# Output projection's first part emitted directly behind the queries' projection; the second gated norm's sums and row placed behind the scores of the second query block

## The chip, the cores and the metric

The kernel runs on one core of one Trainium2 chip. The metric is the device time of one execution in microseconds (us). Five engines of the core matter: TensorE (PE in the profile; its weight loads are PEld), VectorE (DVE), ScalarE (ACT), GpSimd (POOL) and SyncE (SP), which here issues the DMAs.

## The reference

A trunk of two layers over 512 tokens of width 1024, in float32. Each layer: RMSNorm, one input projection, two groups of heads side by side (dilated-window attention with 8 query and 2 key/value heads, and a Mamba-2 scan with 16 heads in 2 groups), one output projection of both results added to the residual; then RMSNorm, a SwiGLU feed-forward and a second addition. The part that the change touches, cut from the mixer:

```python
attn = dilated_attention(q, k, v).reshape(bsz, s, ATTN_WIDTH).astype(h.dtype)
y = ssd_chunked(xs, dt, a_neg, bm, cm) + d_skip.astype(jnp.float32)[:, None] * xs.astype(jnp.float32)
y = y.reshape(bsz, s, SSM_INNER).astype(h.dtype) * jax.nn.silu(z)
gsize = SSM_INNER // SSM_GROUPS
y = rmsnorm(y.reshape(bsz, s, SSM_GROUPS, gsize), ssm_norm.reshape(SSM_GROUPS, gsize))
y = y.reshape(bsz, s, SSM_INNER)
return jnp.concatenate([attn, y], axis=-1) @ w_out
```

The gated norm has two groups of 512 channels, each normalised by itself. The output projection has 1536 rows: 512 of the attention, 512 of the first group and 512 of the second.

## The kernel before

Activations lie transposed: channels on the 128 partitions, the 512 tokens along the free axis. The residual is eight tiles `hT[0..7]` of 128x512. A float32 product is made of three products in a shorter float format: each operand is split in a high part (a cast on ScalarE) and a low part (a subtraction on VectorE), and high by high, low by high and high by low are added up in one PSUM accumulator. `split_x` makes the pair `xh`, `xl` of an activation, `split_w` the pair `whi`, `wlo` of a weight tile. `block` multiplies one weight tile with its activations: 12 products of 512 columns for a tile of the output projection, six in one planner operation.

The order of the work is not the order of the code. The code adds operations to a `Plan`, each with its engine, an estimated duration, the tiles that it reads and writes, and a priority: the value that `at(t)` set last, in estimated us, or for `block` the value of `clock[0]`, which each of its products advances. `schedule` then runs a list schedule with these durations: whenever an engine is free, the ready operation with the lowest priority (then with the lowest number, the order in which it was added) goes next, if the buffers that it opens are to be had. SP takes its loads strictly by priority and number. The instructions are emitted in the resulting order, each engine runs its own in that order, and semaphores are set from the tiles that they share. A dependency that only the planner knows makes no semaphore.

PSUM has three accumulators `acc`, two `hold` and three `tr` for transposes and small products. 56 buffers of 128x512 in SBUF (tag `g`) hold the activations; an operation may not take the last 6 of them if one with a priority lower by over 6 still waits for its first.

A layer goes through: the input projection, with the scan's chunks (`ssd`) and gates (`gate`) of both groups spread over it; the queries' projection, whose end in the program's clock is `tq` (L972); `ssd(1)` and `gate(1, tq + 2)` (L974, L975); the attention, for the query blocks 3, 2, 1, 0 (L1033 to L1035); and the output projection, in three parts of eight blocks each, in the order r = 1 (first scan group), 2 (second scan group), 0 (attention) (L1040). `scores(i, ta)` takes its heads in four pairs: scores of two heads in a `tr` and an `acc`, row minimum with the mask added on VectorE (L1004), exponential with its sum on ScalarE, reciprocal and multiplication on VectorE. `values` transposes the result on TensorE, copies it on ScalarE (`pt`) and multiplies it with the values into a `hold`; at its end the block is split into `ath` and `atl`. Neither of them changes `clock[0]`.

`gate(g, ta)` (L909) multiplies the scan's output with the gate on GpSimd and adds up the squares; `nrm.spread()` (L917) then makes the norm's row: TensorE sums the squares over the partitions (`tr<-ones,sq`), VectorE scales them (`var`), GpSimd takes the power (`rcol`), TensorE transposes the result into a full tile, ScalarE copies it (`rstd`). Four multiplications on GpSimd (`xbc<-xbc,rstd`) apply it, and `split_y` (L921) makes the activations of the projection from them, `xh` on ScalarE and `xl` on VectorE (L435).

Of the kernel before, what the change touches and what calls it, by code (L numbers as in the profile page):

```python
# [15 lines left out]
ALU = mybir.AluOpType  # L16
# [3 lines left out]
P = 128  # L20
# [200 lines left out]
class Plan:  # L221
# [32 lines left out]

    def schedule(self, reserve, near):
# [105 lines left out]
def hybrid_trunk(  # L361
# [105 lines left out]
    def mms(outs, prods, each, prio=None):  # L467

        ins = [v for p in prods for v in p[1:3]]

        def fn():
            for p in prods:
                if len(p) == 3:
                    nc.tensor.transpose(R(p[0]), R(p[1]), R(p[2]))  # L474
                else:
                    nc.tensor.matmul(R(p[0]), R(p[1]), R(p[2]), start=p[3], stop=p[4])  # L476
        plan.add("pe", each * len(prods), outs, ins, fn, prio, lat=0.08)
# [94 lines left out]
    class Norm:  # L572
# [13 lines left out]
        def col(self):  # L586
            t = tr()
            mms([t], [(t[:, i:i + 1], self.ss[:, i * P:(i + 1) * P], ones[:, 0:1], True, True) for i in range(NT)],
                0.45)
            v = small([P, NT], "var", 4)  # L590
# [5 lines left out]
        def spread(self):  # L596
            self.col()
# [50 lines left out]
    def pcol(c):  # L648
        return prm[:, c:c + 1]
# [80 lines left out]
    def layer(l, xs, norm):  # L730
# [178 lines left out]
        def gate(g, ta):  # L909
# [7 lines left out]
            nrm.spread()  # L917
# [17 lines left out]
        gate(0, tx[1] + 2)  # L935
# [39 lines left out]
        gate(1, tq + 2)  # L975
# [58 lines left out]
        for n_, i in enumerate((3, 2, 1, 0)):  # L1034
            values(i, scores(i, ta + 9 * n_), ta + 9 * n_ + 6)  # L1035


        ys = {}
        xs_f, norm_f = [], Norm(KD)
        for r in (1, 2, 0):  # L1040
            if r:
                xo = split_y(r - 1, clock[0] - 6)
            else:
                xo = ats
            po = []
            for c0 in (0, 512):
                if r == 0:
                    wv = w_out[l, 0:512, c0:c0 + 512].rearrange("(v g c) n -> v c g n", v=2, g=4)
                    po += chunk([(slice(v * 64, v * 64 + 64), wv[v]) for v in range(2)], 4, 512)
                else:  # L1050
                    po += rows(w_out[l], r * 512, 4, c0, 512)
            for k in range(KD):
                t = block([(po[k], xo, 0, 4)])
                tt("dve", hT[k], hT[k], t, ALU.add)
                if r == 0:
                    xs_f.append(split_x(hT[k], pcol(PC_FFN + l * 8 + k)))
                    norm_f.square(hT[k])
# [241 lines left out]
```

## Time and profile before

| | us |
|---|---|
| median of 3 runs | 1298.68 |
| lowest, highest | 1298.63, 1300.33 |
| the profiled execution | 1299.57 |
| its span, first to last instruction | 1297.8 |
| TensorE, VectorE busy in the span | 1281.8, 992.2 |
| ScalarE, GpSimd busy in the span | 677.9, 139.2 |

The profile is of one execution, by the hardware profiler. Times count from its first instruction. Busy time is the union of an engine's instructions; matmuls are pipelined and their ends modelled, so TensorE's pace is read better from the starts of successive products. The chain is the work that ended last, followed back from release to release. The mean granted TensorE clock of the execution is 0.998 of full speed.

### The profile page before, as it was taken

The numbers are of one execution on the slowest core, as the hardware profiler recorded it, in microseconds if no ns is written. First come the engines' busy times: TensorE is split into PE (matmuls) and PEld (weight loads), VectorE is DVE, ScalarE is ACT, GpSimd is POOL, SyncE is SP. The second block draws the span as 40 slices with busy tenths as digits, with TensorE's granted clock in tenths as the row PEclk, the third lists the DMA queues.
The fourth block names the chain that finished last, engine by engine and source line by source line (L and its number), as shares of the span: only waits on it lengthen the run. The fifth ranks groups of instructions, "written<-read, shape, count | busy, mean of one in ns | idle before, by whom it ended". The sixth has DMA issues, their size and how long they took to land.

```text
span 1297.8 us, 18639 instructions
## 1 busy us (share of the span) xinstructions
PE 1281.8 (99%) x7316; PEld 1077.6 (83%) x7316; DVE 992.2 (76%) x1678; ACT 677.9 (52%) x1070; POOL 139.2 (11%) x109
## 2 busy tenths in 40 slices
PE   9999999999999999999999999999999999999997
PEld 8877776678889989989888777766788899899896
DVE  7987779668667958959879676886786598597694
ACT  8677656556324524424647686465553244254254
POOL 1013454000000000000000234520000000000000
PEclk9999999999999999999999999999999999999999
DMA  7222221123233233242332222111332432332421
GB/s 242 70 65 66 65 66 65 33 66 98 96 116 113 82 114 98 82 135 70 107 98 78 85 65 65 34 65 33 98 98 82 128 110 80 122 98 74 138 98 65
DMA packets 105736, 115.69 MB, mean 89 GB/s; under 512 B 4656, under 2 KB 95024, under 8 KB 105648
## 3 DMA queue, kind: packets, MB, share of 16 engines
q1 hardware_dynamic: 105504, 114.23, 28.1%
q8 instruction: 58, 0.95, 0.3%
q14 instruction: 30, 0.25, 0.1%
q10 hardware_dynamic: 144, 0.26, 0.1%
HBM read 112.39 MB, written 2.10 MB: 88 GB/s over the span
## 4 chain that ended last, share of the span: by engine, by line
PE 89%; DVE 6%; POOL 1%; ACT 1%; issue 1%; DMA 1%; POOLq 0%; ACTq 0%
PE acc L476 68%; PE hold L476 10%; PE tr L476 7%; PE tr L474 3%; DVE wlo L424 2%; DMA raw<-in_w_up_dram 1%; DVE xbc L435 0%; POOL xbc L424 0%; DVE xl L424 0%; DVE hT L424 0%; DVE sa L430 0%; POOL qr L424 0%; ACT whi L461 0%; DVE xl L435 0%; DVE sa L1004 0%
## 5 line engine op out<-in xcount | busy, mean ns | idle before, releaser
L476 PE MATMUL acc<-xh,whi 128*128 128x512 f32 (+1 forms) x1552 | 562.9, 363 | 3.1 <-DVE hT L424 1.8
L476 PE MATMUL acc<-xl,whi 128*128 128x512 f32 (+1 forms) x1552 | 550.8, 355 | 0.2 <-DVE xl L424 0.2
L476 PE MATMUL acc<-xh,wlo 128*128 128x512 f32 (+1 forms) x1536 | 544.6, 355 | 0.0
L461 ACT CAST whi<-raw 128x1024 fp32r<-128x1024 f32 (+3 forms) x248 | 205.4, 830 | 291.6 <-PE acc L476 266.6
L476 PEld LDWEIGHTS acc<-xh,whi 128*128 128x128 f32 x1552 | 293.8, 189 | 54.2 <-issue 11.8
L476 PEld LDWEIGHTS acc<-xh,wlo 128*128 128x128 f32 x1536 | 290.5, 189 | 42.0 <-DVE wlo L424 0.3
L476 PEld LDWEIGHTS acc<-xl,whi 128*128 128x128 f32 x1552 | 293.9, 189 | 37.3 <-issue 0.7
L424 DVE TENSOR_TENSOR wlo<-raw,whi 128x1024 fp32r<-128x1024 f32 (+2 forms) x240 | 237.4, 994 | 17.6 <-ACT whi L461 17.0
L424 DVE TENSOR_TENSOR hT<-hT,acc 128x512 f32<-128x512 f32 x104 | 71.1, 685 | 110.9 <-PE acc L476 110.2
L461 ACT CAST whi<-wsum 128x1024 fp32r<-128x1024 f32 x64 | 67.2, 1050 | 84.4 <-PE tr L476 40.4
L424 DVE TENSOR_TENSOR wlo<-wsum,whi 128x1024 fp32r<-128x1024 f32 x64 | 78.1, 1221 | 14.3 <-ACT whi L461 14.0
L476 PE MATMUL hold<-xh,wlo 128*128 128x256 f32 x256 | 72.6, 283 | 0.3 <-DVE wlo L424 0.3
L476 PE MATMUL hold<-xh,whi 128*128 128x256 f32 x256 | 72.5, 283 | 0.0
L476 PE MATMUL hold<-xl,whi 128*128 128x256 f32 x256 | 72.4, 283 | 0.0
L594 POOL TENSOR_TENSOR rcol<-var,nhalf 128x4 f32<-128x4 f32 x8 | 8.1, 1018 | 563.6 <-DVE var L430 559.0
L463 ACT ACT_TABLE_LOAD x49 | 62.9, 1283 | 5.0 <-DVE xbc L435 3.0
L435 DVE SCALAR_TENSOR_TENSOR xbc<-cu,prm,xbc 128x511 f32<-128x511 f32 (+2 forms) x72 | 58.2, 815 | 0.8
L463 ACT ACTIVATE sa<-sa,mx 128x512 f32<-128x512 f32 (+3 forms) x64 | 36.0, 563 | 26.2 <-DVE mx L1004 26.2
L476 PEld LDWEIGHTS hold<-xh,wlo 128*128 128x128 f32 x256 | 49.1, 192 | 0.5 <-DVE wlo L424 0.5
L476 PEld LDWEIGHTS hold<-xh,whi 128*128 128x128 f32 x256 | 49.1, 192 | 0.5
L476 PEld LDWEIGHTS hold<-xl,whi 128*128 128x128 f32 x256 | 49.1, 192 | 0.5
L424 DVE TENSOR_TENSOR wsum<-raw 128x512 f32<-128x512 f32 x64 | 42.2, 686 | 1.2 <-DMA raw<-in_w_up_dram 0.9
(231 smaller groups left out, 1834.9 us busy)
## 6 DMA issues: line engine op xcount, KB each, us to landing
raw<-in_w_in_dram SPq DMA_DIRECT2D x24, 1024.0 KB, 5.1
raw<-in_w_gate_dram SPq DMA_DIRECT2D x22, 1024.0 KB, 5.2
raw<-in_w_up_dram SPq DMA_DIRECT2D x22, 1024.0 KB, 5.2
raw<-in_w_down_dram SPq DMA_DIRECT2D x24, 768.0 KB, 4.8
raw<-in_w_out_dram SPq DMA_DIRECT2D x8, 1024.0 KB, 5.1
raw<-in_w_out_dram SPq DMA_DIRECT2D x8, 512.0 KB, 6.5
hT<-in_xT_dram SPq DMA_DIRECT2D x8, 256.0 KB, 4.8
raw<-in_w_down_dram SPq DMA_DIRECT2D x4, 512.0 KB, 3.6
```

Source lines behind the costliest of these rows:

```text
L424: lambda: ENG[eng].tensor_tensor(R(o), R(a), R(b), alu))
L435: lambda: nc.vector.scalar_tensor_tensor(R(o), R(a), R(s), R(b), op0, op1))
L461: nc.scalar.copy(R(o), R(a))
L463: nc.scalar.activation(R(o), R(a), func, **kw)
L474: nc.tensor.transpose(R(p[0]), R(p[1]), R(p[2]))
L476: nc.tensor.matmul(R(p[0]), R(p[1]), R(p[2]), start=p[3], stop=p[4])
L594: lambda: nc.gpsimd.tensor_tensor(R(self.r), R(v), R(nhalf), ALU.pow))
```

## The change

`gate` no longer makes the row; a new function `gated` does, with the four multiplications. The first group calls it at once, as before. For the second group it is called after the scores of the second query block in the order (i = 2), with the priority that stands then (`tq + 16` instead of `tq + 2`), and the planner is told (`follow`) that the sums come behind the last multiplication of these scores. The projection's parts are a function `project(r)`; part r = 1 is called before the attention, the parts 2 and 0 behind it.

```diff
--- before.py
+++ after.py
@@ -251,6 +251,12 @@
             d.users.append(o)
         self.ops.append(o)
         return o
+
+    def follow(self, o, d):
+
+        if d not in o.deps and d is not o:
+            o.deps.add(d)
+            d.users.append(o)
 
     def schedule(self, reserve, near):
 
@@ -474,7 +480,7 @@
                     nc.tensor.transpose(R(p[0]), R(p[1]), R(p[2]))
                 else:
                     nc.tensor.matmul(R(p[0]), R(p[1]), R(p[2]), start=p[3], stop=p[4])
-        plan.add("pe", each * len(prods), outs, ins, fn, prio, lat=0.08)
+        return plan.add("pe", each * len(prods), outs, ins, fn, prio, lat=0.08)
 
     def load(o, src, kb, eng="sp"):
         plan.add(eng, max(0.47, kb / 351.0), [o], [], lambda: ENG[eng].dma_start(R(o), src), lat=2.0)
@@ -583,18 +589,20 @@
             else:
                 tt(eng, self.ss, self.ss, s, ALU.add)
 
-        def col(self):
+        def col(self, follow=None):
             t = tr()
-            mms([t], [(t[:, i:i + 1], self.ss[:, i * P:(i + 1) * P], ones[:, 0:1], True, True) for i in range(NT)],
+            o = mms([t], [(t[:, i:i + 1], self.ss[:, i * P:(i + 1) * P], ones[:, 0:1], True, True) for i in range(NT)],
                 0.45)
+            if follow is not None:
+                plan.follow(o, follow.tile.writer)
             v = small([P, NT], "var", 4)
             ts("dve", v, t[:, 0:NT], 1.0 / (P * self.n), EPS, ALU.mult, ALU.add)
             self.r = small([P, NT], "rcol", 4)
             plan.add("pool", 0.96, [self.r], [v, nhalf],
                      lambda: nc.gpsimd.tensor_tensor(R(self.r), R(v), R(nhalf), ALU.pow))
 
-        def spread(self):
-            self.col()
+        def spread(self, follow=None):
+            self.col(follow)
             t = tr()
             tposes(t, [(t[:, i * P:(i + 1) * P], self.r[:, i:i + 1].broadcast_to([P, P]), ident) for i in range(NT)])
             self.row = G("rstd")
@@ -914,7 +922,10 @@
                 act(z[j], z[j], AF.Silu)
                 tt("pool", xbc[j], xbc[j], z[j], ALU.mult)
                 nrm.square(xbc[j], E_ADD)
-            nrm.spread()
+            return nrm
+
+        def gated(g, nrm, follow=None):
+            nrm.spread(follow)
             for j in range(g * 4, g * 4 + 4):
                 tt(E_ROW, xbc[j], xbc[j], nrm.row, ALU.mult)
 
@@ -932,7 +943,7 @@
             for i in range(4):
                 z[g * 4 + i] = scaled(block([(pz[i], xs, 0, KD)]), "z")
         ssd(0, tx[0], tx[1])
-        gate(0, tx[1] + 2)
+        gated(0, gate(0, tx[1] + 2))
 
 
         A = {"q": []}
@@ -972,7 +983,30 @@
         tq = clock[0]
 
         ssd(1, tx[1] + 3, tq)
-        gate(1, tq + 2)
+        nrm1 = gate(1, tq + 2)
+
+
+        xs_f, norm_f = [], Norm(KD)
+
+        def project(r):
+            if r:
+                xo = split_y(r - 1, clock[0] - 6)
+            else:
+                xo = ats
+            po = []
+            for c0 in (0, 512):
+                if r == 0:
+                    wv = w_out[l, 0:512, c0:c0 + 512].rearrange("(v g c) n -> v c g n", v=2, g=4)
+                    po += chunk([(slice(v * 64, v * 64 + 64), wv[v]) for v in range(2)], 4, 512)
+                else:
+                    po += rows(w_out[l], r * 512, 4, c0, 512)
+            for k in range(KD):
+                t = block([(po[k], xo, 0, 4)])
+                tt("dve", hT[k], hT[k], t, ALU.add)
+                if r == 0:
+                    xs_f.append(split_x(hT[k], pcol(PC_FFN + l * 8 + k)))
+                    norm_f.square(hT[k])
+        project(1)
 
 
         ats = []
@@ -1032,29 +1066,13 @@
 
         ta = tq
         for n_, i in enumerate((3, 2, 1, 0)):
-            values(i, scores(i, ta + 9 * n_), ta + 9 * n_ + 6)
-
-
-        ys = {}
-        xs_f, norm_f = [], Norm(KD)
-        for r in (1, 2, 0):
-            if r:
-                xo = split_y(r - 1, clock[0] - 6)
-            else:
-                xo = ats
-            po = []
-            for c0 in (0, 512):
-                if r == 0:
-                    wv = w_out[l, 0:512, c0:c0 + 512].rearrange("(v g c) n -> v c g n", v=2, g=4)
-                    po += chunk([(slice(v * 64, v * 64 + 64), wv[v]) for v in range(2)], 4, 512)
-                else:
-                    po += rows(w_out[l], r * 512, 4, c0, 512)
-            for k in range(KD):
-                t = block([(po[k], xo, 0, 4)])
-                tt("dve", hT[k], hT[k], t, ALU.add)
-                if r == 0:
-                    xs_f.append(split_x(hT[k], pcol(PC_FFN + l * 8 + k)))
-                    norm_f.square(hT[k])
+            pr = scores(i, ta + 9 * n_)
+            if n_ == 1:
+                gated(1, nrm1, pr[-1])
+            values(i, pr, ta + 9 * n_ + 6)
+
+        for r in (2, 0):
+            project(r)
 
 
         at(clock[0])
```

## Rows read from the trace of the kernel before

**Rows 1.** The page: busy us (share) xinstructions; the chain's shares by engine.
```profile
PE 1281.8 (99%) x7316; PEld 1077.6 (83%) x7316; DVE 992.2 (76%) x1678; ACT 677.9 (52%) x1070; POOL 139.2 (11%) x109
...
PE 89%; DVE 6%; POOL 1%; ACT 1%; issue 1%; DMA 1%; POOLq 0%; ACTq 0%
```

**Rows 2.** Windows: stretch, length, busy us (instructions) of PE, PEld, DVE, ACT, POOL; clock.
```profile
203.00:217.00 14.00, 12.39 (x66) 8.92 (x66) 13.41 (x29) 9.93 (x20) 8.06 (x7) 1.00 0.16 62
217.00:240.00 23.00, 23.00 (x132) 15.17 (x131) 17.20 (x57) 14.63 (x38) 0.00 (x0) 1.00 0.15 46
240.00:256.00 16.00, 16.00 (x88) 10.67 (x87) 10.74 (x43) 9.79 (x30) 0.00 (x0) 1.00 0.31 68
```

**Rows 3.** Timeline of TensorE: start us, us, operation, xcount [idle before <-releaser].
```profile
203.04 0.94 PE L476 MATMUL tr<-ones,sq 128*128 128x1 f32 x8
204.37 0.50 PE L476 MATMUL acc<-xh,whi 128*128 128x512 f32 x1 [0.38 <-DVE mx L1004]
204.71 0.40 PE L476 MATMUL acc<-xl,whi 128*128 128x512 f32 x1
...
205.63 0.39 PE L476 MATMUL acc<-xh,wlo 128*128 128x512 f32 x1
205.95 0.50 PE L476 MATMUL tr<-kh,xh 64*128 64x512 f32 x1
206.66 0.50 PE L476 MATMUL acc<-kh,xh 64*128 64x512 f32 x1 [0.21 <-DVE hT L424]
207.27 0.49 PE L476 MATMUL tr<-kh,xl 64*128 64x512 f32 x1
...
207.92 0.50 PE L476 MATMUL acc<-xh,whi 128*128 128x512 f32 x1
```

**Rows 4.** Timeline of TensorE: four transposes and the product behind them, both layers.
```profile
214.34 0.66 PE L474 MATMUL tr<-ident,sa 128*128 128x128 f32 x4
215.90 0.50 PE L476 MATMUL acc<-xh,whi 128*128 128x512 f32 x1 [0.91 <-DVE hT L424]
...
230.55 0.66 PE L474 MATMUL tr<-ident,sa 128*128 128x128 f32 x4
230.96 0.47 PE L476 MATMUL acc<-xh,whi 128*128 128x512 f32 x1
...
856.86 0.50 PE L476 MATMUL acc<-xh,whi 128*128 128x512 f32 x1 [0.92 <-DVE hT L424]
```

**Rows 5.** Timeline of VectorE: first addition of the projection, fourth query block read.
```profile
196.93 0.69 DVE L424 TENSOR_TENSOR hT<-hT,acc 128x512 f32<-128x512 f32 x1 [0.24 <-PE acc L476]
...
198.31 0.68 DVE L435 SCALAR_TENSOR_TENSOR qr<-acc,rstd 128x512 f32<-128x512 f32 x1
```

**Rows 6.** Timeline of VectorE: the norm's var and the low parts.
```profile
207.13 0.15 DVE L430 TENSOR_SCALAR var<-tr 128x4 f32<-128x4 f32 x1
...
213.47 1.78 DVE L435 SCALAR_TENSOR_TENSOR xl<-xbc,prm,xh 128x512 fp32r<-128x512 f32 x1
...
217.91 1.41 DVE L435 SCALAR_TENSOR_TENSOR xl<-xbc,prm,xh 128x512 fp32r<-128x512 f32 x2
```

**Rows 7.** Timeline of GpSimd: the norm's power and its four multiplications.
```profile
207.36 1.02 POOL L594 TENSOR_TENSOR rcol<-var,nhalf 128x4 f32<-128x4 f32 x1 [2.30 <-DVE den L1008]
210.72 5.67 POOL L424 TENSOR_TENSOR xbc<-xbc,rstd 128x512 f32<-128x512 f32 x4 [2.33 <-ACT rstd L461]
```

**Rows 8.** Timelines: block two's last multiplication on VectorE, part 2's first product on TensorE.
```profile
237.07 0.42 DVE L430 TENSOR_SCALAR sa<-sa,den 128x384 f32<-128x384 f32 x1
...
239.72 0.47 PE L476 MATMUL acc<-xh,whi 128*128 128x512 f32 x1
```

**Rows 9.** Timeline of ScalarE: the norm's row copied, the first high part.
```profile
210.05 0.59 ACT L461 COPY rstd<-tr 128x512 f32<-128x512 f32 x1
...
212.05 0.72 ACT L463 ACTIVATE xh<-xbc,prm 128x512 fp32r<-128x512 f32 x1 [0.22 <-POOL xbc L424]
```

**Rows 10.** Groups of TensorE from 239.7 to 252.7: one form of three.
```profile
L476 PE MATMUL acc<-xh,whi 128*128 128x512 f32 x10 | 4.2, 421 | 0.0
```

## The prediction

> **What bounds the kernel now.** I read the page's busy times first, then the chain that ended last, and then the stretches around the moved code. TensorE is busy 99% of the span and is 89% of the chain [rows 1]. A moved step is therefore worth only the time in which TensorE stands still, or in which it changes between kinds of product. The reader is to see next that the place of the old norm is where VectorE is full: 13.41 of 14 us from 203 to 217, with TensorE at 12.39 of 14, while from 217 to 240 and from 240 to 256 VectorE has 5.8 and 5.3 us to spare and TensorE none [rows 2]. Both layers run this stretch alike, the second 640.95 us later (stalls at 215.90 and 856.86 [rows 4]), so everything below is counted per layer and doubled.
>
> **Part one, the first part of the projection.** In the planner an operation is ordered by its priority, and for these blocks that is the TensorE clock of the program, which neither `scores` nor `values` advances. The clock at which part 1 was emitted in the old loop is thus the one right after the queries' projection, as in the new place. The trace agrees: the first addition of a block into hT is at 196.93, before the accumulator of the fourth query block has even been read (198.31) [rows 5]. Only the numbers that decide ties change; there is one equal priority, the first six products of part 1 against the first scores. Its weight loads keep their priorities as well, so no DMA passes another on SP's queue. I cost this part at 0; its bound is one such group exchanged with its neighbour, six products that start 0.23 us apart (four of them from 204.71 to 205.63 [rows 3]), 1.4 us either way.
>
> **Part two, what leaves the old place.** Eight records of the sums (0.94 us at 203.04), the row's transposes, VectorE's var, GpSimd's power (1.02) and four multiplications (5.67 together), ScalarE's copy of the row and four casts, and VectorE's four `xl` [rows 3, 6, 7]. The queues behind them: GpSimd does nothing else from 217 to 256 [rows 2], so its five instructions pass nobody there; SP has no part in them.
>
> (a) The stall at 215.90. VectorE's first `xl` takes 1.78 us where the next two take 1.41 together, until 215.25 [rows 6], and the addition into hT, which sets an accumulator free, stands behind it on VectorE. TensorE's next product waits for that addition [rows 4]. From the four transposes at 214.34 to the product at 215.90 pass 1.56 us; the same pair of steps at 230.55 takes 0.41 [rows 4]. Loss 1.15 us, and it should go, since `xl` leaves this place: -1.15, bounded by 0 if another VectorE instruction takes its turn. What is late next there are scores' own row minima and multiplications, and VectorE, relieved of some 4 us, has them earlier.
>
> (b) The stall at 205.95. Six score products in pairs should take three steps of 0.33, as 207.27 to 207.92 does for two, so 0.98; they took 1.97, because the accumulator waited for hT's addition and the next pair for a query block's `xl` [rows 3]. None of that work is moved. I take 0; the bounds are 0 and -1.0.
>
> (c) The sums' own time. At the old place the product behind them waits another 0.38 us for a row minimum [rows 3], so without the sums TensorE reaches that wait earlier and gains nothing, whereas at the new place, where it is never idle, they cost what they last. +0.94, bounded by 0 if they fall into a wait again. The transposes of the row, four as short as those at 230.55, cost the same in both places: 0.
>
> (d) The new wait. The old order left the second part of the projection long slack: the second and third `xl` are done at 219.32, its first product runs at 239.72 [rows 6, 8]. Now the sums are ordered behind the last multiplication of the second query block's scores, which ended at 237.49 [rows 8]; it may come some 2 us earlier by (a) and by the rooms that the sums and the row no longer take in the scarce transposing buffers. From sums to the second `xl` is a chain: 0.94 + 0.15 + 1.02 + 0.41 + 0.59 + two multiplications of 1.42 + 0.72 + 0.71 = 7.4 us without any handing over [rows 3, 4, 6, 7, 9], and 16.3 as it ran before (203.04 to 219.32). So the first product of part 2 can come between 243 and 254, instead of 239.7. In the 13 us from 239.7 part 2 had 30 products (ten of each of three forms), 0.23 us apart 6.9 us [rows 10]; that is what TensorE lacks if nothing replaces it, the upper bound. What replaces it are the scores of the third query block and the values of the second, which ran between them before, and the last blocks of part 1, which yield to scores that are ready earlier. I take a little, +0.4, because ready attention work is there for most of the gap; bounds 0 and +6.9. Whether the cover is enough hangs on VectorE and ScalarE, which from 240 to 256 are at 10.74 and 9.79 of 16 [rows 2].
>
> (e) Changes of kind. A plain product starts 0.23 us after its like, but scores with 64 rows start 0.32 us after a plain product (205.63 to 205.95 [rows 3]): 0.1 us for a passage, which I take for both directions. With part 2 held back, attention pieces stand side by side, and my estimate is two visits to plain products less, four passages: -0.4, bounds 0 and -0.8.
>
> GpSimd's multiplications hold up VectorE: beside them an `xl` took 1.78 us, after them 0.71 each, 1.07 us lost [rows 6]. The Trainium skill (SBUF — State Buffer, Who interferes with whom) says that a VectorE instruction with two operands in SBUF waits for a GpSimd instruction that reads SBUF, the one that started first keeping the ports to its end. By that rule the 1.07 us is moved with the multiplications, onto the chain of (d), and (d) would be +1.4, the total 2.0 us more; by the row alone it could be the full queue of the old place that made `xl` long. The trace leans to the rule, which makes the second rival dearer.
>
> Sum per layer: 0 - 1.15 + 0 + 0.94 + 0.4 - 0.4 = -0.21, for two layers -0.4. The profiled execution took 1299.57 (span 1297.8 and 1.8 around it), so 1299.15 in its place; the median of the runs is 0.89 below the profiled one, which gives 1298.3.
>
> **The rivals.** *It helps.* VectorE's relief also takes half of (b), the sums fall into a wait and nothing is waited for in (d): -1.15 - 0.5 - 0.4 = -2.05 per layer, -4.1 in all, 1294.6. For it: VectorE is at 96% in the old place and near 70% in the new [rows 2]. Against it: (b) happens before the first instruction that leaves VectorE, `var` at 207.13 [rows 6].
>
> *It hurts.* TensorE's order is written by the planner, with durations of its own; if GpSimd, ScalarE and VectorE bring `xl` later than the planner thought, the first product of part 2 stands in its place and everything behind it waits. That products wait in order is seen at 206.66, where scores wait for an addition and all behind them with it [rows 3]. Price: half of the 6.9 us, 3.4, in place of the 0.4: -1.15 + 0.94 + 3.4 - 0.4 = +2.8 per layer, 5.6 in all, 1304.3. It decides from 1.9 us of waiting per layer on (then the sum is +2.6). For it: 20 us of slack turn into nearly none. Against it: attention work ran without an idle moment between the products of part 2. The Trainium skill (TensorE: Matmul & The Clock Gate, Step-by-step: what each phase is for) has it that the queue pulls only weight loads ahead and keeps the matmuls in program order; the row at 206.66 agrees.
>
> *It does nothing.* Part one is a renumbering, and of part two the planner's new order ends level to within a few tenths: 1298.7. The first is nearly certain by [rows 5], the second a matter of luck.
>
> **How the numbers follow.** Forecast 0.38, no effect 0.08, it helps 0.29, it hurts 0.25. From no change a measurement of this kernel can tell about 0.2%, 2.6 us (its three runs lie 1.7 us apart). Forecast and no effect lie within that, the other two outside: faster 0.29, same 0.46, slower 0.25. Range: (a) whole, (b) gone and (c) hidden give, with (e), -2.55 per layer, 1293.6; the hurting case reaches 1304.3, and its bound of +6.9 goes far beyond. I leave a tenth out on each side: 1293.6 to 1304.5. The likeliest's own range is 1296 to 1301.
>
> **What would show it.** The sums should stand behind the last 384-column multiplication, at some 235 to 238, in the trace. Right for (a): no idle of 0.9 us before a product near 215, and VectorE from 203 to 217 below 12 us. For (b): the pair at 206 still slow. For (d): the start of part 2's first product against the end of part 1's last addition, and TensorE's idle between 238 and 252; more than 1.9 us in each layer shows the hurting rival. The forecast falls if TensorE's idle changes elsewhere, where this change should reach nothing.

## The result, and the profile after

| | before | after |
|---|---|---|
| median of the runs, us | 1299.51 (4 runs) | 1307.78 (4 runs) |
| lowest to highest | 1298.63 to 1302.46 | 1305.76 to 1309.12 |
| the profiled execution, its span | 1299.57, 1297.8 | 1307.41, 1305.6 |

The ratio is 1.0058, with the interval [1.0044, 1.0071]: the change costs some 8 us. It lies above the forecast of 1298.3 and above the whole range, which ended at 1304.5. Lines are 6 higher in the helpers of the changed kernel (the product L476 is L482, `xl` L435 is L441) and the row minimum L1004 is L1038.

The page after, the rows that answer to [rows 1]: the same numbers of instructions, with busy times within 2 us of those before, in a span 7.8 us longer.

```profile
PE 1281.8 (98%) x7316; PEld 1077.1 (82%) x7316; DVE 990.3 (76%) x1678; ACT 678.0 (52%) x1070; POOL 138.3 (11%) x109
...
PE 90%; DVE 6%; DMA 1%; ACT 1%; issue 1%; POOL 1%; POOLq 0%; ACTq 0%
```

The windows of [rows 2], after (columns as there):

```profile
203.00:217.00 14.00, 11.81 (x50) 8.51 (x48) 10.85 (x26) 6.58 (x14) 2.62 (x2) 0.88 0.20 75
217.00:240.00 23.00, 23.00 (x133) 15.13 (x132) 15.89 (x58) 15.93 (x42) 0.00 (x0) 1.00 0.14 46
240.00:256.00 16.00, 13.50 (x76) 8.37 (x76) 11.18 (x37) 9.68 (x25) 6.50 (x5) 1.00 0.01 2
```

VectorE is relieved in the first window, as forecast (10.85 for 13.41), and yet TensorE got through 50 records in place of 66 there (twelve of the 66 are the sums and the row's transposes, which moved); in the third 76 in place of 88. Two places, then, not one. What TensorE waited for between 185 and 285 (in all, times, longest), after and then before:

```profile
PE acc L482 <- DVE hT L430: 2.2, 1, 2.2
PE acc L482 <- DVE xl L441: 2.0, 2, 1.3
PE tr L480 <- DVE sa L436: 0.5, 1, 0.5
PE tr L482 <- DVE xl L430: 0.4, 1, 0.4
```

```profile
PE acc L476 <- DVE hT L424: 1.1, 2, 0.9
PE acc L476 <- DVE mx L1004: 0.4, 1, 0.4
```

**The first place.** TensorE before, the first score product; then after, the same product, the waits for a query block's `xl` and for `hT`, and the wait for `hT` of layer 1:

```profile
190.25 0.50 PE L476 MATMUL tr<-kh,xh 64*128 64x512 f32 x1
```

```profile
193.28 0.49 PE L482 MATMUL tr<-kh,xh 64*128 64x512 f32 x1
...
201.87 0.50 PE L482 MATMUL tr<-kh,xl 64*128 64x512 f32 x1 [0.42 <-DVE xl L430]
...
203.82 0.39 PE L482 MATMUL acc<-xh,wlo 128*128 128x512 f32 x1
206.40 0.50 PE L482 MATMUL acc<-xh,whi 128*128 128x512 f32 x1 [2.19 <-DVE hT L430]
...
207.50 0.63 PE L482 MATMUL acc<-xh,whi 128*128 128x512 f32 x1
207.92 0.63 PE L482 MATMUL acc<-xl,whi 128*128 128x512 f32 x1
...
849.52 0.50 PE L482 MATMUL acc<-xh,whi 128*128 128x512 f32 x1 [2.00 <-DVE hT L430]
```

Before, the first pair of scores ran at 190.25, behind six products of 512 columns; now it runs behind eighteen, 3.03 us later. From 203.82 to 206.40 pass 2.58 us where a step between such products takes 0.23: 2.35 lost. Behind this standstill seven products start 0.43 us apart, 0.20 lost with each, 1.40. In layer 1 the standstill is there too (2.17 lost between 847.13 and 849.52), but not the slow products.

**The second place.** TensorE, GpSimd and VectorE after, around part 2's first products:

```profile
239.66 0.95 PE L482 MATMUL tr<-ones,sq 128*128 128x1 f32 x8
240.54 1.09 PE L482 MATMUL hold<-pt,vk 128*64 128x512 f32 x4
...
246.50 0.49 PE L482 MATMUL acc<-xh,whi 128*128 128x512 f32 x1
248.29 0.50 PE L482 MATMUL acc<-xl,whi 128*128 128x512 f32 x1 [1.29 <-DVE xl L441]
...
249.99 0.50 PE L482 MATMUL acc<-xl,whi 128*128 128x512 f32 x1 [0.73 <-DVE xl L441]
...
251.52 0.33 PE L480 MATMUL tr<-ident,sa 128*128 128x128 f32 x1 [0.47 <-DVE sa L436]
```

```profile
241.19 1.02 POOL L602 TENSOR_TENSOR rcol<-var,nhalf 128x4 f32<-128x4 f32 x1 [34.65 <-DVE var L436]
243.90 5.48 POOL L430 TENSOR_TENSOR xbc<-xbc,rstd 128x512 f32<-128x512 f32 x4 [1.68 <-ACT rstd L467]
```

```profile
246.48 1.75 DVE L441 SCALAR_TENSOR_TENSOR xl<-xbc,prm,xh 128x512 fp32r<-128x512 f32 x1
...
248.75 1.18 DVE L441 SCALAR_TENSOR_TENSOR xl<-xbc,prm,xh 128x512 fp32r<-128x512 f32 x1
...
251.38 0.74 DVE L441 SCALAR_TENSOR_TENSOR xl<-xbc,prm,xh 128x512 fp32r<-128x512 f32 x1
```

Over the usual steps TensorE loses 1.56, 0.90 and 0.64 us here, 3.10 in layer 0, and 3.08 in layer 1. The first two losses are waits for part 2's `xl`, 2.46 together; the third is a wait for a multiplication `sa` of the third query block.

**Where the time went.** The same instruction of the scan or of the projection, start after minus start before, is the measure: +0.30 ahead of layer 0's attention, +5.22 behind its output projection, +3.69 ahead of layer 1's attention, +5.82 behind its projection, +7.76 in the feed-forward of layer 1. So the mixer of layer 0 costs 4.92 us: 2.35 and 0.58 (a wait for a query block's `xl` at 201.87) and 1.40 at the first place, 3.10 at the second, less 2.57 for the stalls of before (0.52, 0.71, 0.27 and 1.07), which are gone; that makes 4.86. Layer 1's costs 2.13: 2.17 and 3.08 less 2.90, 2.35. The -1.5 between them is a stretch from 773 to 777 in which the trace of before has its products at half rate, and that of after has not; the +1.9 at the end are waits for the low parts of weights (1.16 at 1040.83). Neither of these two follows the change: of the experiments' profiles some have them and some have not. Nor does the 1.40 of slow products belong to the change for certain, since experiment 3's trace has the same wait at the same place and no slow products.

### The profile page after: what moved, and what is told of

Same layout as the page of the kernel before. It is cut to its first block, busy times and chain, and to the rows that moved or that the text cites. A ratio compares the mean times of both kernels' runs of the same rounds, so it can differ in the third digit from the quotient of the medians.

```text
span 1305.6 us, 18639 instructions
## 1 busy us (share of the span) xinstructions
PE 1281.8 (98%) x7316; PEld 1077.1 (82%) x7316; DVE 990.3 (76%) x1678; ACT 678.0 (52%) x1070; POOL 138.3 (11%) x109
## 4 chain that ended last, share of the span: by engine, by line
PE 90%; DVE 6%; DMA 1%; ACT 1%; issue 1%; POOL 1%; POOLq 0%; ACTq 0%
PE acc L482 69%; PE hold L482 10%; PE tr L482 8%; PE tr L480 3%; DVE wlo L430 1%; DMA raw<-in_w_up_dram 1%; DVE xl L441 1%; DVE xbc L441 0%; DVE sa L1038 0%; DMA w<-in_w_in_dram 0%; POOL xbc L430 0%; DVE sa L436 0%; DVE xl L430 0%; POOL sq L430 0%; ACT whi L467 0%
## 5 line engine op out<-in xcount | busy, mean ns | idle before, releaser
L482 PE MATMUL acc<-xh,whi 128*128 128x512 f32 (+1 forms) x1552 | 562.8, 363 | 4.3 <-DVE hT L430 4.2
L482 PE MATMUL acc<-xl,whi 128*128 128x512 f32 (+1 forms) x1552 | 552.0, 356 | 4.3 <-DVE xl L441 4.0
L482 PE MATMUL acc<-xh,wlo 128*128 128x512 f32 (+1 forms) x1536 | 545.3, 355 | 0.0
L482 PEld LDWEIGHTS acc<-xh,whi 128*128 128x128 f32 x1552 | 294.2, 190 | 55.2 <-issue 9.7
L482 PEld LDWEIGHTS acc<-xl,whi 128*128 128x128 f32 x1552 | 294.3, 190 | 43.2 <-DVE xl L441 5.5
L482 PEld LDWEIGHTS acc<-xh,wlo 128*128 128x128 f32 x1536 | 290.9, 189 | 41.5 <-DVE wlo L430 0.3
L482 PE MATMUL hold<-xh,wlo 128*128 128x256 f32 x256 | 72.8, 284 | 1.8 <-DVE wlo L430 1.8
L482 PE MATMUL hold<-xh,whi 128*128 128x256 f32 x256 | 72.5, 283 | 0.0
L482 PE MATMUL hold<-xl,whi 128*128 128x256 f32 x256 | 72.4, 283 | 0.0
L441 DVE SCALAR_TENSOR_TENSOR xbc<-cu,prm,xbc 128x511 f32<-128x511 f32 (+2 forms) x72 | 58.2, 815 | 0.8
L482 PEld LDWEIGHTS hold<-xh,wlo 128*128 128x128 f32 x256 | 49.1, 192 | 2.4 <-DVE wlo L430 2.4
L482 PEld LDWEIGHTS hold<-xh,whi 128*128 128x128 f32 x256 | 49.1, 192 | 0.5
L482 PEld LDWEIGHTS hold<-xl,whi 128*128 128x128 f32 x256 | 49.1, 192 | 0.5
```

Source lines behind the costliest of these rows:

```text
L441: lambda: nc.vector.scalar_tensor_tensor(R(o), R(a), R(s), R(b), op0, op1))
```

## The experiments

All in five rounds, each with its own runs of the kernel before beside it (medians 1299.3 to 1300.3). Times in us; "layer 0" is the shift against before behind that layer's output projection.

**1. The two parts by themselves.** Part one alone (the norm's row stays in its old place); diff against the changed kernel:

```diff
-        nrm1 = gate(1, tq + 2)
+        gated(1, gate(1, tq + 2))
...
-            if n_ == 1:
-                gated(1, nrm1, pr[-1])
```

> The changed kernel with the second group's row made at once, as before: only part one of the change. The theory of the late row (the 7.8 us come from part 2's low parts, which stand 3.1 us of waiting in each layer in TensorE's way) expects the time of the kernel before, ratio 0.999 to 1.001 to it, and sums at about 203 as before. The rival, that part one alone already costs (the first score pair goes behind 12 plain products, 193.3 instead of 190.3, and an addition into hT comes 2.2 us late at 204), expects TensorE waiting 2 us for hT near 204 and 847 and a ratio of 1.001 to 1.004.

Part two alone:

```diff
-        project(1)
...
-        for r in (2, 0):
+        for r in (1, 2, 0):
```

> The changed kernel with the projection's three parts in one loop behind the attention, as before: only part two of the change. Late row: two waits for xl near 247 and 889, 3.1 us lost per layer, the stall at 215 gone (1.1 won back) and sums and row (1.3) no longer in a pause: about +3 per layer, ratio 1.004 to 1.006. Part one as the cause: no such waits, ratio near 1.000.

Part one alone: 1311.04, ratio 1.0087 [1.0073, 1.0100], slower than both parts together. Part two alone: 1304.59, 1.0029 [1.0019, 1.0038]. So the part that I had costed at nothing is the dearer one. Not all of its 11 us are waits: in its profile two stretches of layer 0, from 208.5 to 211.9 and from 222.1 to 225.5, have a granted clock of 0.50, where the changed kernel has one. Its waits from 185 to 285:

```profile
PE acc L482 <- DVE hT L430: 3.2, 2, 1.8
PE tr L480 <- DVE mx L1038: 0.9, 1, 0.9
PE tr L482 <- DVE xl L430: 0.4, 1, 0.4
```

What part one is can be read from the planner's orders. If in this kernel the first pair of scores alone gets a priority 0.001 lower, the planner puts out the instructions of the kernel before, the same on all five engines; the same edit in the changed kernel gives those of part two alone. The whole of part one is thus one equal priority, which the number of the operation decides: part 1's first six products change places with the first pair of scores, six of a query block that stood behind the pair are now ahead of it as well, and from there on the planner's orders part.

**2. The row, not waited for.** The four multiplications write a tile that nobody reads, so the second group is left without its norm:

```diff
-                tt(E_ROW, xbc[j], xbc[j], nrm.row, ALU.mult)
+                tt(E_ROW, xbc[j] if g == 0 else G("dm"), xbc[j], nrm.row, ALU.mult)
```

> The changed kernel, but the four multiplications of the second group write into a tile that nobody reads: the row is made at the same late place and its work stays on every engine, but part 2 of the projection does not wait for it (it leaves out the second group's norm). Late row: the waits for xl near 247 and 889 vanish, 3.1 us per layer, so 6 us below the changed kernel, ratio to the kernel before 1.000 to 1.002. If instead the moved work itself (GpSimd holding up VectorE, the sums in a full stretch of TensorE) cost the time, it stays at 1.004 to 1.006.

1305.46, 1.0036 [1.0024, 1.0049]. In layer 0 the shift falls to +0.77, with the wait for `hT` (2.1) left and none for `xl`. Behind layer 1's projection it is +4.96, but +4.08 of that has come up ahead of its attention, in the scan, where the granted clock is 0.50 from 812.3 to 815.7; so the attention and projection of layer 1 add only 0.9, although a second such stretch, from 849.9 to 853.3, lies in them. The planner arranged its order anew for this edit, so the price is not clean; experiment 8 has it cleaner.

**3. The row one query block earlier**, in the changed kernel:

```diff
-            if n_ == 1:
+            if n_ == 0:
```

> The changed kernel with the sums and the row placed behind the scores of the first query block instead of the second, some 12 us earlier. Late row: the chain from the sums to the second low part took 9 to 10 us, so xl are there before part 2 begins at about 240 and nothing waits for them: 6 us below the changed kernel, ratio to the kernel before 0.998 to 1.002. If the place beside the attention is the cost wherever it lies, the waits move with it and the ratio stays above 1.004.

1300.12, 1.0004 [0.9994, 1.0015], level with before. No `xl` of part 2 is waited for; the wait for `hT` is as long as ever (2.2). With the row earlier the waits for `xl` go and the time with them: the lateness of the row is a cost that can be avoided, though the planner's order is another one here too.

**4. Both mended**: part two alone with the row behind the first block (the edits of 1 and 3).

> Part two alone (part 1 of the projection is emitted behind the attention as in the kernel before, so the first pair of scores goes ahead of part 1's products), with the second group's row placed behind the scores of the first query block instead of the second. Theory of two separate costs (the exchange at the first scores, and the late row): neither is left, the row is early enough that part 2's first xl is not awaited, and the old stalls near 216 go as they did in part two alone (-2.65 by the end of part 1): about -2.3 per layer, 1294 to 1297, with the kernel before near 1300. Rival (the exchange cost nothing once the row had left its old place, so that the changed kernel with the row behind the first block, 1300.1, is already what this gives): 1300, within 1 us of the kernel before, and new waits near 216 or 240 in place of the old ones.

1301.92, 1.0013 [1.0004, 1.0022]: the theory missed by 5 us. Where the waits for `xl` and the old stalls are gone there are others, 1.9 for row minima and 0.4 for `rcol`. It also showed a misreading of mine: the -2.65 "by the end of part 1", on which its forecast was built, is no time won. The planner had put part 1's end ahead of score work, which then came later; only the shift behind the whole projection counts (+1.19 here in layer 0).

**5. The row's multiplications on VectorE** (`E_ROW if g == 0 else "dve"`), in part two alone and in the changed kernel. Part two alone is made here, and in experiment 6, by `clock[0] += 1e-3` in front of `project(1)`, which decides the tie as before; without the other edit it gives the orders of part two alone.

> Part two alone as in the run of that name (row behind the scores of the second query block, 1304.6, first scores ahead of part 1), but the second group's four multiplications with the row run on VectorE instead of GpSimd. Theory (the waiting for part 2's xl is the length of the chain from the sums, above all four GpSimd multiplications of 1.2 to 1.7 us and an xl of 1.75 us beside them): with about 0.7 each on VectorE the second xl comes 2 to 3 us earlier, the wait for xl of 2.0 us falls under 0.5, and about 2 us per layer are won: 1300 to 1301. Rival (VectorE is full, so that four multiplications more delay score and addition instructions by what they last): the wait for xl goes, but others of the same size come, 1304 to 1306.

> The changed kernel with the second group's four multiplications with the row on VectorE instead of GpSimd; the exchange at the first scores stays. Theory of two costs: the wait for xl (about 3.1 us lost per layer) falls to under 1, the stall near 204 and 847 of 2.2 us stays, about -2.3 per layer: 1302 to 1304, against 1307.8 of the changed kernel. Rival (one cause, VectorE too late throughout, which four instructions more make worse): 1307 to 1310, with longer waits for row minima and hT additions.

1306.01, 1.0050 [1.0037, 1.0062], and 1308.60, 1.0063 [1.0050, 1.0076]. The wait for `xl` falls to 0.3, as the chain says, but in the first kernel 1.9 for row minima and 0.6 for `xh` take its place, in the second 0.8 and 0.6: the times are the rivals'.

**6. The sums early, the row late**: part two alone without the dependency on the scores (`gated(1, nrm1)`).

> Part two alone without the planner's dependency of the sums on the scores: the sums stand at their old place in TensorE's order, the row's transposes and all behind them keep the late priority. Theory (only the lateness of the row costs, and it comes from the dependency and its chain): the row's multiplications start before 240, no xl of part 2 is awaited, the old stall at 206 stays and the one at 216 goes: about -1 per layer, 1297 to 1299. Rival (the gain in part two alone up to the end of part 1, 2.65 us, came from taking the sums out of their old place): no gain at that point, 1300.

1305.33, 1.0044 [1.0031, 1.0057]; no `xl` is waited for, and 2.0 for row minima are. Both its theory and its rival were too low: every new order so far brings a wait on VectorE of the size of the one that it removes.

**7. VectorE's load and TensorE's order.** The eight multiplications of the first query block on ScalarE, in the changed kernel, in the kernel before, and in that of experiment 3:

```diff
-                ts(E_SC, sa[:, 0:nk], sa[:, 0:nk], d, None, ALU.mult)
+                if i == 3:
+                    act(sa[:, 0:nk], sa[:, 0:nk], AF.Copy, scale=d)
+                else:
+                    ts(E_SC, sa[:, 0:nk], sa[:, 0:nk], d, None, ALU.mult)
```

> The changed kernel with the eight multiplications by the reciprocal sum of the first query block on ScalarE instead of VectorE (some 0.5 to 1.5 us each; eight fewer on VectorE per layer). Theory (the exchange at the first scores costs because VectorE, filled with its own queue around 196 to 206, brings the accumulator's hT addition too late): the wait for hT of 2.2 us falls under 1 us, the half clock behind it in layer 0 goes, the waits for xl near 246 stay: about -2.5 to -3.5 in layer 0 and -1.5 in layer 1, 1303 to 1305 against 1307.8. Rival (the wait comes from TensorE's new order alone, which spends its plain products early, and not from VectorE's load): the wait stays near 2 us, 1307 to 1309.

> The kernel before with the same eight multiplications on ScalarE, alone. Theory (its own waits in that place, 0.52, 0.71, 0.27 and 1.07 us lost per layer, are VectorE's load): about half of these 2.6 us go, 1296 to 1298, a version faster than both. Rival (ScalarE, 9.9 of 14 us busy there, now brings exponentials and casts late, or the row minima and not the multiplications are what is late): 1299 to 1302.

> The changed kernel with the row behind the first query block's scores (1300.1 as it ran) and these eight multiplications on ScalarE. Theory (its one long wait is that for hT, 2.2 us per layer): 1296 to 1299. Rival (the wait only moves on to the next row minimum): 1300 to 1302.

And the kernel before with the scores still further ahead (`clock[0] += 1.3` in front of its projection):

> The kernel before with all three parts of the projection 1.3 us of the planner's clock later (the length of six products), so that the scores go further ahead of part 1, the opposite of the exchange that the changed kernel makes. Theory (what counts is that VectorE has score work early, since it is the full engine until 217): no later than the kernel before, 1297 to 1300. Rival (any other order than that of the kernel before only exchanges waits, and its own is a lucky one): 1301 to 1306, with waits for hT or row minima longer than the 2.6 us of before.

Changed kernel: 1306.35, 1.0053 [1.0040, 1.0066]; the wait for `hT` is 2.4, not shorter, which is the rival's sign, though the time lies between the two. Kernel before: 1298.69, 0.9989 [0.9980, 0.9998], a little faster than without. Experiment 3's: 1305.16, 1.0034 [1.0021, 1.0047], worse than without and above both expectations, with 4.0 us of waits for `hT`. Scores further ahead: 1306.88, 1.0057 [1.0045, 1.0070], with one wait of 3.1 for a multiplication `sa`. That is above the rival's range too. So scores early are no good in themselves, and my theory that VectorE must have score work early falls with that run. VectorE ahead of the late addition, in the changed kernel with the multiplications on ScalarE:

```profile
198.17 1.53 DVE L430 TENSOR_TENSOR wlo<-raw,whi 128x512 fp32r<-128x512 f32 x1
...
200.83 1.77 DVE L430 TENSOR_TENSOR xl<-qr,xh 128x512 fp32r<-128x512 f32 x1
...
203.77 1.45 DVE L430 TENSOR_TENSOR qr<-qr,cosT 128x512 f32<-128x512 f32 x1
205.14 0.67 DVE L430 TENSOR_TENSOR hT<-hT,acc 128x512 f32<-128x512 f32 x1
```

There are fewer instructions on VectorE, but others are long now (`wlo` took 1.18 there in the changed kernel). That pointed to GpSimd, which runs beside them.

**8. The same order, without GpSimd's work.** An operation is planned as ever and then not issued, so TensorE, VectorE, ScalarE and SP keep their order to the instruction. The waits for its results go with it. Left out are, in the first kernel, the rotary work of the last two query blocks and the second group's gates and square sums (`xbc*z`, `sq+sq`); in the second, the four multiplications with the row; in the third, both; the fourth is the kernel before without the first set.

```diff
+        drop = eng == "pool" and omit[0]
         plan.add(eng, dcost(eng, o, [a, b]), [o], [a, b],
-                 lambda: ENG[eng].tensor_tensor(R(o), R(a), R(b), alu))
+                 lambda: None if drop else ENG[eng].tensor_tensor(R(o), R(a), R(b), alu))
```

> The changed kernel with every instruction of VectorE, TensorE and ScalarE in the same order, but without GpSimd's work of the stretch from 190 to 208: it leaves out the rotary multiplication and addition of the last two query blocks and the gates' multiplications and square sums of the second group. Theory A (the hT addition awaited near 204 is late because VectorE's instructions ahead of it are stretched beside GpSimd's: 1.48 for a multiplication that takes 0.47, 1.78 for one that takes 0.67): the wait of 2.2 us falls under 0.7, the half clock behind it goes, the waits for xl near 246 stay: -3 in layer 0, -1.5 in layer 1, 1303 to 1304 against 1307.8. Theory B (VectorE idles before the late scores and the addition stands behind them in its queue, whatever their lengths): the wait falls by less than 0.7, 1306 to 1308.

> The changed kernel with every instruction of TensorE, VectorE, ScalarE in the same order, but without the second group's four GpSimd multiplications with the row (left out, so that the second group is not normalised). Theory (they and the xl stretched beside them are the last link before part 2's products): the waits at 246 to 252 of 3.1 us per layer go, to under 0.5, the stall near 204 and 847 stays: 1301.5 to 1303 against 1307.8. Rival (VectorE's own queue holds up xl there): the waits stay over 1.5 us, 1305 to 1307.

> The changed kernel with both left out, in the same order: GpSimd's work of the stretch and the second group's multiplications with the row. If the two costs add, as the theory of two separate causes has it: 1297 to 1299, level with the kernel before (about 1300) or a little under. If one only moves into the other: 1301 or more.

> The kernel before, in its order, without the same GpSimd work of the stretch (rotary of the last two query blocks, the second group's gates and square sums). It shows what that work costs in the order of before: by theory A its waits there (0.52, 0.71, 0.27, 1.07 us lost per layer) fall by half, 1296 to 1298 against about 1300; by theory B they stay, 1299 to 1300.

| left out | time | against its own kernel | ratio to before |
|---|---|---|---|
| stretch, in the changed order | 1301.94 | -5.8 (1307.78) | 1.0019 [1.0010, 1.0028] |
| row, in the changed order | 1304.47 | -3.3 | 1.0034 [1.0022, 1.0046] |
| both, in the changed order | 1298.85 | -8.9 | 0.9992 [0.9983, 1.0000] |
| stretch, in the order of before | 1297.11 | -3.2 (1300.27) | 0.9976 [0.9966, 0.9987] |

5.8 and 3.3 are 9.1 and both together 8.9: as far as medians of runs that spread by 3 to 5 us can tell, the two costs add. The first time lies below theory A's range, the second between the theory and its rival, the third and the fourth within what the theories gave. Of the waits of the kernel before from 185 to 285 only one for `hT` is left (0.9 at 214.26, behind an `xl` of 1.77 beside the row's multiplications). VectorE in the changed kernel and then in the first of these, the same instructions in the same order (whose helpers' lines are 2 higher still), and last GpSimd in the changed kernel:

```profile
196.54 1.48 DVE L436 TENSOR_SCALAR sa<-sa,den 128x512 f32<-128x512 f32 x1
197.95 0.67 DVE L430 TENSOR_TENSOR hT<-hT,acc 128x512 f32<-128x512 f32 x1
...
200.31 1.50 DVE L430 TENSOR_TENSOR xl<-qr,xh 128x512 fp32r<-128x512 f32 x1
...
203.36 1.78 DVE L430 TENSOR_TENSOR qr<-qr,cosT 128x512 f32<-128x512 f32 x1
...
205.67 0.68 DVE L430 TENSOR_TENSOR hT<-hT,acc 128x512 f32<-128x512 f32 x1
```

```profile
196.29 0.48 DVE L438 TENSOR_SCALAR sa<-sa,den 128x512 f32<-128x512 f32 x1
...
198.94 0.68 DVE L432 TENSOR_TENSOR xl<-qr,xh 128x512 fp32r<-128x512 f32 x1
...
201.15 0.69 DVE L432 TENSOR_TENSOR qr<-qr,cosT 128x512 f32<-128x512 f32 x1
...
203.28 0.69 DVE L432 TENSOR_TENSOR hT<-hT,acc 128x512 f32<-128x512 f32 x1 [0.83 <-PE acc L484]
```

```profile
196.45 1.30 POOL L430 TENSOR_TENSOR qr<-qr,qs 128x512 f32<-128x512 f32 x1
197.69 1.49 POOL L430 TENSOR_TENSOR xbc<-xbc,z 128x512 f32<-128x512 f32 x1
199.98 1.29 POOL L430 TENSOR_TENSOR sq<-sq,sq 128x512 f32<-128x512 f32 x1 [0.80 <-ACT sq L469]
203.23 1.35 POOL L430 TENSOR_TENSOR qs<-qs,sinT 128x512 f32<-128x512 f32 x1 [1.96 <-DVE qs L954]
```

Three instructions give back 2.9 us, and the addition comes 2.4 us earlier: it now starts as soon as its own products end, after 0.83 us in which VectorE waits for them. TensorE's next product still waits for it:

```profile
204.03 0.50 PE L484 MATMUL acc<-xh,whi 128*128 128x512 f32 x1 [0.78 <-DVE hT L432]
```

So of the wait of 2.2 some 0.8 is the new order's own, in which the next product needs the accumulator whose products have just ended, and 1.4 is VectorE's delay. The waits of TensorE from 185 to 285, first without the stretch's work, then without the row's:

```profile
PE acc L484 <- DVE xl L443: 2.0, 2, 1.3
PE acc L484 <- DVE hT L432: 0.8, 1, 0.8
PE tr L482 <- DVE sa L438: 0.5, 1, 0.5
```

```profile
PE acc L484 <- DVE hT L432: 2.2, 1, 2.2
PE acc L484 <- DVE xl L443: 0.6, 2, 0.3
PE tr L482 <- DVE sa L438: 0.5, 1, 0.5
PE tr L484 <- DVE xl L432: 0.4, 1, 0.4
```

Each omission takes away its own wait and leaves the other. The wait for `hT` fell by 1.4, theory A's side, though to 0.8 and not under 0.7; the loss behind the row fell from 3.10 to 1.64, where I had expected the waits under 0.5. Of the 1.64, 0.64 is the wait for `sa`, as long as before; the waits for `xl` lose 1.0 in place of 2.46. Whether that 1.0 is the length of the chain from the sums or VectorE's queue is not shown.

**9. Had back with nothing left out?** The rotary multiplication and addition of the last two query blocks on VectorE, in the kernel before; then the same with experiment 7's multiplications on ScalarE:

```diff
-            tt("pool", s, s, sinT, ALU.mult)
+            tt(eng, s, s, sinT, ALU.mult)
...
-            tt(E_ROT, r, r, s, ALU.add)
+            tt(eng, r, r, s, ALU.add)
...
-            qq = rotary(block([(pq[i], xs, 0, KD)]), -0.125)
+            qq = rotary(block([(pq[i], xs, 0, KD)]), -0.125, "dve" if i > 1 else "pool")
```

> The kernel before with the rotary multiplication and addition of the last two query blocks on VectorE (about 0.68 each) instead of GpSimd (1.25 to 1.3 each), nothing left out. If the stretching beside GpSimd is what is lost there (3.2 us over both layers without GpSimd's work, four of some eleven instructions per layer of which are these), VectorE gives 4 times 0.68 per layer and gets back some 2 us: level or up to 1.5 us faster, 1298 to 1300. If VectorE's fullness decides, it is slower: 1301 to 1304.

> The same with the first query block's multiplications by the reciprocal sum on ScalarE (1298.7 with these alone on the kernel before), so that VectorE's load in the stretch is what it was. If both help independently: 1296.5 to 1298. If the planner's new order brings a wait of its own: 1300 to 1303.

Alone 1308.44, 1.0061 [1.0046, 1.0075], above both expectations. VectorE is busy 7.00 of 7 us from 190 to 197 and 6.72 from 197 to 204, and TensorE does 5.39 in the second. But VectorE's fullness is not shown to be all of it: TensorE's longest waits in layer 0 are 1.7 for a row minimum, 1.6 for GpSimd's sum of squares and 1.1 for its power, and the granted clock is 0.50 from 213.5 to 216.9 and from 845.0 to 851.8. With the load evened out 1298.14, 0.9982 [0.9973, 0.9991], some 2 us faster than before and 9 to 10 than the changed kernel: the fastest version that leaves nothing out, though its interval overlaps that of experiment 7's 1298.69.

## Why the prediction was wrong, step by step

**Part one, costed at 0: this step failed.** It said that only the numbers that decide ties change, that there is one equal priority, and that its bound is six products exchanged, 1.4 us either way. The tie is the right one, and no other priority moved. But a tie is not worth the length of what is exchanged. Twelve products went ahead of the scores, six of them not even part 1's; the scores came 3.03 us later, and everything that the planner laid out from there on is another order, in which TensorE needs an accumulator that has only just been filled (0.8 of the wait of 2.2) and VectorE has the addition that frees it behind stretched instructions (1.4). The price is 2.35 and 0.58 in layer 0, with 1.40 of slow products behind them in this execution, and 2.17 in layer 1, for the 0; alone, where sums and row stay in their old place, 11 us.

**(a) -1.15, right.** At the old place the product now follows the four transposes by 0.35 (215.16 to 215.51); [rows 4] had 1.56. What I had not asked is whether part one's new wait takes the relief away again, as it did.

**(b) 0, bounds 0 and -1.0: at its bound.** The slow pairs (0.71 and 0.27) are gone, and so is the 0.52 behind the old sums; an earlier pair waits for a query block's `xl` now, the 0.58 counted under part one. My argument, that none of the work there is moved, held for the work and not for its order.

**(c) +0.94, right in part two alone.** At the new place the sums last from 239.66 to the next record at 240.54, 0.88, with no wait ahead of them. At the old place part two alone gains nothing by their absence: its wait for the row minimum is 1.18 in place of 0.38, as (c) said. In the changed kernel the wait there is the one for `hT`, and how much of its 2.35 the missing sums make is not split.

**(d) +0.4, mis-sized: it measured 3.1.** The rival "it hurts" had 3.4 and the point of 1.9 from which it decides; part two alone measured 1304.59 against its 1304.3, though a stretch at a granted clock of 0.50 (247.0 to 250.4) is in that too. The cover that I took for granted was attention work standing ready. It covers TensorE without a gap from the sums to 246.50; then part 2's first products stand next in TensorE's order, and what comes behind them waits with them, as that rival said. Nor did the multiplication that the sums follow come the 2 us earlier that I allowed: it ended at 237.51, before at 237.49. The rule of the Trainium skill (SBUF — State Buffer, Who interferes with whom), which the prediction weighed as +1.0, is borne out: `xl` took 1.75 at 246.48 beside the multiplications and 0.74 behind them, 1.0 apart.

**(e) -0.4: not seen.** The items above leave 0.06 in layer 0 and -0.22 in layer 1 for it and all else.

The sum failed on two of its small terms: 0 and +0.4 stood for +4.3 and +3.1 in layer 0 and for +2.2 and +3.1 in layer 1. Both prices hang in part on what GpSimd does beside VectorE: leaving its work out in the stretch is worth 5.8 in the new order and 3.2 in the old, so 2.6 of the 8 us are that difference. Leaving out the row's multiplications is worth 3.3 in the new order, but not all of that is new: in the old order too an `xl` is long beside them (1.78, [rows 6]) and TensorE waits behind it. No run leaves the row out there, so how the other 5 us divide between the row's place and the new order stays open, and so does why one order meets GpSimd's work better than another.

## What to carry to other kernels

Where a planner's list decides the order, a change of numbering is a change of schedule: emit both, compare the orders engine by engine, and price the first difference by what waits behind it, not by its length. To tell order from load, keep the order and leave single instructions out; moving work anywhere else makes the planner deal all cards anew. And count time won only behind the last step that the reordered work shares.

## What the runs showed of the hardware

A VectorE instruction beside GpSimd's can take two to three times as long: `sa` 1.48 for 0.48, `xl` 1.50 for 0.68, `qr` 1.78 for 0.69. Not every one does: `hT<-hT,acc`, which reads one operand from PSUM, takes its usual 0.67 at 197.95, beside GpSimd's `xbc` from 197.69 to 199.18. In the changed kernel, taking eight instructions off VectorE handed the stretching to others. The Trainium skill (SBUF — State Buffer, Who interferes with whom) says that a VectorE instruction with two operands in SBUF contends with a GpSimd one that reads SBUF, and one in a two-port mode too, which can take in `sa` with its one; the rows agree.

After some standstills of TensorE the granted clock is at the lower level, 1.2 GHz: in the changed kernel it is 0.51 from 206.73 to 210.06. Windows of that kernel, before and behind the end of the wait (columns as in [rows 2]):

```profile
200.00:206.40 6.40, 3.79 (x18) 2.05 (x16) 6.40 (x11) 1.24 (x2) 3.75 (x3) 1.00 0.38 142
206.40:210.10 3.70, 3.70 (x10) 2.88 (x11) 2.37 (x6) 1.62 (x5) 0.14 (x1) 0.56 0.10 38
```

TensorE was busy 3.79 of 6.40 us ahead of the fall, and 512-column products start 0.43 apart at the lower level, 0.23 at the upper: 1.40 us here, on top of a wait of 2.2. A standstill alone doesn't foretell it: 2.17 lost at 847.13 in the same trace, and 2.55 at 846.70 in the changed kernel with ScalarE's multiplications, were followed by full speed. Nor do the us ahead of it: in experiment 3's trace TensorE was busy 3.80 of the same 6.40 us, waited 2.21 at 206.43, and then ran at a granted clock of 1.00 from 206.40 to 210.10. What tells these cases apart stays open.
